# Sliding-window attention on one core: one TensorE visit per query tile, scores on row halves

## The chip, the cores and the metric

The kernel runs on one core of a Trainium2 chip. The metric is the device time of one execution in microseconds (us). TensorE (PE) takes its instructions in the order in which they are recorded; each engine has such a queue of its own, and engines wait for one another by semaphores.

## What is computed

One step of a two-layer decoder trunk: layer 0 is a gated linear recurrence, layer 1 sliding-window attention with sinks. The change touches layer 1 alone. Its core in the reference:

```python
def sink_attention(q, k, v, mask, sinks):
    s = jnp.einsum('bnqhgd,bnshd->bnhgqs', q, k) * SWA_SCALE
    s = jnp.where(mask[None, :, None, None], s, -jnp.inf)
    sink = sinks.astype(jnp.float32)[None, None, :, :, None, None]
    m = jnp.maximum(jnp.max(s, axis=-1, keepdims=True), sink)
    p = jnp.exp(s - m)
    p = p / (jnp.sum(p, axis=-1, keepdims=True) + jnp.exp(sink - m))
    return jnp.einsum('bnhgqs,bnshd->bnqhgd', p, v)
```

There are 32 query heads of 64 dimensions and 4 key heads. The prompt has 272 positions (16 of them meta tokens) with a window of 128; the sample group has 8 sequences of 8 new positions, each against 128 cached keys and its own 8. All numbers are f32. Layer 1 projects to q, k, v and a gate (2048 x 4608), attends, multiplies by SiLU of the gate and projects back.

## The kernel before, in words

`Stream` records the whole program in one order. Its main loop (`run`) goes through the weight matrices in tiles of 128 output columns, each tile in 4 chunks of 4 weight blocks. For each block it records three projection matmuls (L212 to L214: low weights by high inputs, high by low, high by high, all at full f32r rate) and then calls `step`, which advances at most two of the waiting side chains. A side chain is a Python generator: `yield 4` means that its next part is recorded 4 steps later at the earliest. So everything that is not a projection is strewn between the projections, at distances given by these yields. A tile is 16 steps, or 48 projection matmuls.

Weights come by DMA on the SP queue, 512 KB for two chunks, up to 14 chunks ahead (`raw`); ScalarE makes the rounded high part (L158), VectorE the rest (L169). Those conversions are recorded some chunks ahead.

In layer 1 the tiles are k0, k1, v0, v1, 16 query tiles (two heads each), 16 gate tiles. When query tile j is through, `epi_qq` starts `prompt_chain(j)`: `unfold` (scale and shift), a split into f32r parts `qh`, `ql`, three matmuls each for the first 128 queries (`sa`, 2 x 144 keys) and the others (`sb`, 2 x 256 keys), `softmax` on VectorE and ScalarE, eight transposes of the probabilities (L1056 to L1060), copies to SBUF (`t1`, `t2`), the outputs (`ao`, L1071 to L1077) and a copy into `oT`. The two heads of a tile share one key head; so that one matmul gives both heads' scores over all 128 rows, `kzh`, `kzl`, `knz`, `kzs` hold the keys twice, padded with zeros: half 0 on rows 0 to 63, half 1 on rows 64 to 127. Chains of neighbouring tiles overlap in time.

Twice per group of four tiles (one key head q), `sample_chain(q, u)` handles four of the eight sequences: it loads cached keys `cd` and values `cv`, transposes the keys (`ck`), copies them to `kzs`, computes scores (`ss`), softmax, transposes the probabilities (`st`) and makes outputs (`so`).

`tile_position` names the part of the 128 x 128 array that a matmul uses: `(0, 64 * h)` a half of its columns, `(0, 32 * i)` a quarter of them, `(64 * h, 0)` a half of its rows. A row half has its own 64 rows of weights and input and writes to a PSUM bank of its own. f32 matmuls run as two passes and appear as two instructions each. `pj`, `lv`, `mm` are the PSUM pools, with 3, 2 and 3 banks. `L["att"]` counts chains that run; the gate chains wait for it to be zero before they use `oT`.

## Time and profile before

| | |
|---|---|
| median of 3 runs | 1191.69 us (1191.45 to 1192.14) |
| profiled execution | 1193.07 us, span from first to last instruction 1191.3 us |
| granted TensorE clock, mean | 0.991 |
| instructions profiled | 26295, of them 10163 matmuls |

How to read it: the span is split by engine into busy times. Weight loads (PEld) overlap matmuls. A row of the timeline has the start from the beginning of the span, the length, engine, line, operation, tile written and tiles read, rows * columns of the array, shape and count of merged neighbours; in brackets the engine's idle time ahead and what ended it. Buffer numbers are left out of names.

### The profile page before, as it was taken

The page shows a single profiled execution, that of the slowest core. Times are in us where ns is not written, and L with a number is a line of the kernel's source. Part 1 is how long each engine was busy: PE and PEld are TensorE (multiplying, and loading weights), DVE is VectorE, ACT ScalarE, POOL GpSimd, SP SyncE. Part 2 cuts the span into 40 slices and gives each one's busy share as a digit, 9 for nine tenths or more (in the row PEclk, how much of TensorE's full clock was granted, in tenths as well). Part 3 has the DMA queues.
Part 4 walks back from the last instruction along what each step waited for, and adds up shares of the span by engine and source line. Part 5 has one row for each costly group of instructions (what it writes and reads, how often), then busy time and mean ns, then how long its engine had stood idle before and what let it go on. Part 6 is the DMA issues. An engine that isn't in the chain of part 4 may idle for free.

```text
span 1191.3 us, 26295 instructions
## 1 busy us (share of the span) xinstructions
PE 1170.4 (98%) x10163; PEld 1125.5 (94%) x10163; DVE 792.3 (67%) x2049; ACT 609.9 (51%) x1779; POOL 236.8 (20%) x350
## 2 busy tenths in 40 slices
PE   9999999999999999999999999999999999999995
PEld 7999999999999999999999999988888899999994
DVE  3765666565666565566578777678777767777675
ACT  4655545545555545555444446666656655553340
POOL 3022212212212212212224332000000011144420
PEclk8999999999999999999999999999999999999997
DMA  9545655445655545655455555634244345555532
GB/s 260 145 128 159 178 146 145 138 134 160 180 145 146 138 133 161 179 145 151 136 146 145 143 146 166 180 103 129 74 116 117 89 126 162 151 151 178 144 93 89
DMA packets 328462, 171.47 MB, mean 144 GB/s; under 512 B 19085, under 2 KB 325613, under 8 KB 328167
## 3 DMA queue, kind: packets, MB, share of 16 engines
q1 hardware_dynamic: 327792, 168.82, 50.2%
q8 instruction: 80, 1.31, 0.5%
q0 software_dynamic: 544, 0.97, 0.2%
q14 instruction: 46, 0.37, 0.1%
HBM read 156.97 MB, written 14.42 MB: 144 GB/s over the span
## 4 chain that ended last, share of the span: by engine, by line
PE 92%; issue 3%; DVE 2%; DMA 1%; ACT 1%; POOL 1%; SPq 0%; POOLq 0%; DVEq 0%; ACTq 0%
PE pj_q L212 7%; PE pj_g L212 7%; PE pj_g L213 7%; PE pj_g L214 6%; PE pj_q L213 6%; PE pj_q L214 6%; PE pj_f L212 4%; PE pj_i L212 3%; PE pj_i L214 3%; PE pj_i L213 3%; PE pj_f L214 3%; PE pj_f L213 3%; PE pj_z L214 3%; PE pj_z L213 3%; PE pj_z L212 3%
## 5 line engine op out<-in xcount | busy, mean ns | idle before, releaser
L212 PE MATMUL pj_q<-xh,wlo_q 128*128 128x336 f32 (+1 forms) x512 | 166.6, 325 | 0.0
L212 PE MATMUL pj_g<-xh,wlo_g 128*128 128x336 f32 (+1 forms) x512 | 162.9, 318 | 0.0
L213 PE MATMUL pj_q<-xl,whi_q 128*128 128x336 f32 (+1 forms) x512 | 161.2, 315 | 0.0
L214 PE MATMUL pj_q<-xh,whi_q 128*128 128x336 f32 (+1 forms) x512 | 160.9, 314 | 0.0
L213 PE MATMUL pj_g<-xl,whi_g 128*128 128x336 f32 (+1 forms) x512 | 160.6, 314 | 0.0
L214 PE MATMUL pj_g<-xh,whi_g 128*128 128x336 f32 (+1 forms) x512 | 160.4, 313 | 0.0
L212 PEld LDWEIGHTS pj_q<-xh,wlo_q 128*128 128x128 f32 x512 | 97.1, 190 | 5.8 <-issue 4.7
L212 PEld LDWEIGHTS pj_g<-xh,wlo_g 128*128 128x128 f32 x512 | 96.6, 189 | 1.5 <-issue 1.3
L213 PEld LDWEIGHTS pj_q<-xl,whi_q 128*128 128x128 f32 x512 | 97.3, 190 | 0.5
L214 PEld LDWEIGHTS pj_q<-xh,whi_q 128*128 128x128 f32 x512 | 97.1, 190 | 0.0
L213 PEld LDWEIGHTS pj_g<-xl,whi_g 128*128 128x128 f32 x512 | 96.8, 189 | 0.1
L214 PEld LDWEIGHTS pj_g<-xh,whi_g 128*128 128x128 f32 x512 | 96.6, 189 | 0.0
L169 DVE TENSOR_TENSOR wlo_g<-raw_g,whi_g 128x512 fp32r<-128x512 f32 x128 | 90.4, 743 | 0.6 <-ACT whi_g L158 0.6
L169 DVE TENSOR_TENSOR wlo_q<-raw_q,whi_q 128x512 fp32r<-128x512 f32 x128 | 85.1, 684 | 5.3 <-ACT whi_q L158 5.3
L212 PE MATMUL pj_f<-xh,wlo_f 128*128 128x336 f32 x256 | 83.7, 327 | 0.0
L213 PE MATMUL pj_f<-xl,whi_f 128*128 128x336 f32 x256 | 81.5, 318 | 0.0
L214 PE MATMUL pj_f<-xh,whi_f 128*128 128x336 f32 x256 | 81.5, 318 | 0.0
L212 PE MATMUL pj_i<-xh,wlo_i 128*128 128x336 f32 x256 | 81.4, 318 | 0.0
L212 PE MATMUL pj_z<-oh,wlo_z 128*128 128x336 f32 x256 | 81.3, 317 | 0.0
L214 PE MATMUL pj_z<-oh,whi_z 128*128 128x336 f32 x256 | 81.1, 317 | 0.0
L213 PE MATMUL pj_z<-ol,whi_z 128*128 128x336 f32 x256 | 81.0, 316 | 0.0
L213 PE MATMUL pj_i<-xl,whi_i 128*128 128x336 f32 x256 | 80.9, 316 | 0.0
(401 smaller groups left out, 3161.2 us busy)
## 6 DMA issues: line engine op xcount, KB each, us to landing
raw_g<-in_hgrn_w_in_dram SPq DMA_DIRECT2D x32, 512.0 KB
raw_z<-in_hgrn_w_out_dram SPq DMA_DIRECT2D x32, 512.0 KB
raw_q<-in_swa_w_in_dram SPq DMA_DIRECT2D x32, 512.0 KB
raw_g<-in_swa_w_in_dram SPq DMA_DIRECT2D x32, 512.0 KB
raw_y<-in_swa_w_out_dram SPq DMA_DIRECT2D x32, 512.0 KB
raw_f<-in_hgrn_w_in_dram SPq DMA_DIRECT2D x30, 512.0 KB
raw_q<-in_hgrn_w_in_dram SPq DMA_DIRECT2D x30, 512.0 KB
raw_i<-in_hgrn_w_in_dram SPq DMA_DIRECT2D x30, 512.0 KB
```

What stands on the lines that cost most here:

```text
L169: e.nc.vector.tensor_tensor(lo, t.pop(("raw", kc)), hi.bitcast(F32), op=ALU.subtract)
L212: nc.tensor.matmul(ps, lo[:, kk, :], xh, start=first, stop=False)
L213: nc.tensor.matmul(ps, hi[:, kk, :], xl, start=False, stop=False)
L214: nc.tensor.matmul(ps, hi[:, kk, :], xh, start=False, stop=last)
```

## The change

`prompt_chain` and `sample_chain` are gone. In their place stands `query_chain`, which after unfold and split makes one `visit(n)`. A visit records, one behind the other on TensorE: the scores of tile n, the transposes of the probabilities of tile n-1, transposes for a sample group if `plan` has some there (cached keys, or sample probabilities), the outputs of tile n-2 and sample outputs. Behind it come the softmax of n (`softmax_chain`) and the copies out of PSUM. After the last tile four visits (n = 16 to 19) finish the rest among the gate projections.

Keys are no longer padded: each half of the rows holds its own copy, and scores are pairs of matmuls, half h for head h, into two banks. Sample scores use eight parts of 64 rows by 32 columns. `vm0` has 128 rows (112 of them zero) instead of 16, `vs` 128 for each half instead of 64, so that all outputs use 128 rows by 64 columns; `t2` becomes two fixed tiles whose lower part is zeroed once. The sample probabilities lie in 384 neighbouring columns, three transposes instead of four. `ck` and `st` come from pool `pj` instead of `mm`. The yields in `softmax` are 3 and 3.

```diff
-            for nm, shape in (("vm1", [P, 256]), ("vm2", [P, 256]), ("vm0", [16, 256]), ("vs", [NS, 256]),
+            for nm, shape in (("vm1", [P, 256]), ("vm2", [P, 256]), ("vm0", [P, 256]), ("vs", [P, 2, 256]),
                               ("km2", [P, 256]), ("ks", [NS, 256]),
                               ("sk", [P, 32]), ("sks", [P, 8])):
                 L[nm] = ap1.tile(shape, F32, tag=nm, name=nm)
+            for q in range(2):
+                L["t2", q] = ap1.tile([P, 512], F32, tag=f"t2_{q}", name=f"t2_{q}")
+            for t in (L["vm0"], L["vs"], L["t2", 0][:, 256:512], L["t2", 1][:, 256:512]):
+                nc.gpsimd.memset(t, 0.0)
...
             for q in range(4):
                 for nm in ("kzh", "kzl"):
-                    t = ap1.tile([P, 2, NP], F32R, tag=f"{nm}{q}", name=f"{nm}{q}")
-                    L[nm, q] = t
-                t = ap1.tile([P, 2, NS], F32, tag=f"knz{q}", name=f"knz{q}")
-                nc.gpsimd.memset(t, 0.0)
-                L["knz", q] = t
+                    L[nm, q] = ap1.tile([P, NP], F32R, tag=f"{nm}{q}", name=f"{nm}{q}")
+                L["knz", q] = ap1.tile([P, NS], F32, tag=f"knz{q}", name=f"knz{q}")
                 L["qs", q] = ap1.tile([P, 8, 4, 8], F32, tag=f"qs{q}", name=f"qs{q}")
             for q in range(2):
-                t = ap1.tile([P, 4, 2, P], F32, tag=f"kzs{q}", name=f"kzs{q}")
-                nc.gpsimd.memset(t, 0.0)
-                L["kzs", q] = t
-            def zeros():
-                yield 20
-                for q in range(4):
-                    for nm in ("kzh", "kzl"):
-                        nc.scalar.copy(L[nm, q][0:64, 1, :], zero[0:64, :])
-                        nc.scalar.copy(L[nm, q][64:128, 0, :], zero[64:128, :])
-                        yield 4
-            st.spawn(zeros())
+                L["kzs", q] = ap1.tile([P, 4, P], F32, tag=f"kzs{q}", name=f"kzs{q}")
...
-            yield 4
+            yield 3
             for c, pt in enumerate(parts):
...
-            yield 3 if nm is not None else 4
+            yield 3
...
-            yield 5 if nm is not None else 4
...
-        def prompt_chain(j, pq):
+        def query_chain(j, pq):
...
+            yield from visit(j, (qh, ql))
+            if j == KT - 1:
+                for n in range(KT, KT + 4):
+                    yield (8, 1, 4, 1)[n - KT]
+                    yield from visit(n)
+                L["att"] = 0
+        plan = {}
+        for q in range(4):
+            for u in range(2):
+                n = 4 * q + 3 + u
+                plan.setdefault(n - 1, {})["load"] = q, u
+                plan.setdefault(n, {})["keys"] = q, u
+                plan.setdefault(n + 2 - u * (q == 3), {})["trans"] = q, u
+                plan.setdefault(n + 3 - u * (q == 3), {})["out"] = q, u
+        plan[18]["trans"] = 3, 1
+        plan[17]["trans"] = 3, 0
+        plan[18]["out"] = 3, 0
+        plan.setdefault(19, {})["out"] = 3, 1
+        def visit(n, qq=None):
+            ap = L["ap"]
+            todo = plan.get(n, {})
+            while 0 < n <= KT and ("p", n - 1) not in L:
+                yield 0
+            while "trans" in todo and ("sp",) + todo["trans"] not in L:
+                yield 0
+            if n < KT:
+                qh, ql = qq
+                kh, kl = L["kzh", n // 4], L["kzl", n // 4]
+                pa = [lv.tile([P, 512], F32, tag="lv", name=f"s{c}{n}") for c in "ab"]
+                for o, w, t0, k0 in ((0, 144, 0, 0), (144, 256, 128, 16)):
+                    for i, (a, b) in enumerate(((ql, kh), (qh, kl), (qh, kh))):
+                        for h in range(2):
+                            r = halves2[h]
+                            nc.tensor.matmul(pa[h][:, o:o + w], a[r, t0:t0 + 128], b[r, k0:k0 + w], start=i == 0,
+                                             stop=i == 2, tile_position=(64 * h, 0), skip_group_check=True)
+            j = n - 1
+            if 0 <= j < KT:
+                sm = L["p", j]
+                p1, p2 = pm(f"p1_{j}"), pm(f"p2_{j}")
+                for h in range(2):
+                    nc.tensor.transpose(p1[:, 256 * h:256 * h + 128], sm[:, h, 16:144], ident)
+                    nc.tensor.transpose(p1[:, 256 * h + 128:256 * h + 256], sm[:, h, 144:272], ident)
+                for h in range(2):
+                    nc.tensor.transpose(p2[:, 128 * h:128 * h + 128], sm[:, h, 272:400], ident)
+                    nc.tensor.transpose(p2[0:16, 256 + 128 * h:384 + 128 * h], sm[:, h, 0:16], ident)
+            px = None
+            for kind in ("keys", "trans"):
+                if kind in todo:
+                    q, u = todo[kind]
+                    px = e.pj.tile([P, 512], F32, tag="pj", name=f"{'ck' if kind == 'keys' else 'st'}{q}_{u}")
+                    if kind == "keys":
+                        cd = L["cd", u]
+                        for i in range(4):
+                            nc.tensor.transpose(px[:, 128 * i:128 * i + 128], cd[:, i].rearrange("p h d -> p (h d)"),
+                                                ident)
+                    else:
+                        for i in range(3):
+                            nc.tensor.transpose(px[:, 128 * i:128 * i + 128],
+                                                L["sp", q, u][:, 128 * i:128 * i + 128], ident)
+            po = None
+            j2 = n - 2
+            if j2 >= 0:
+                po = pm(f"ao{j2}")
+            if 0 <= j2 < KT:
+                vs = slice(64 * (j2 // 4), 64 * (j2 // 4) + 64)
+                t1, t2 = L["t1", j2], L["t2", j2 % 2]
+                for v, t, c0, o, w in (("vm1", t1, 0, 0, 256), ("vm2", t2, 0, 128, 128), ("vm0", t2, 256, 0, 128)):
+                    for h in range(2):
+                        nc.tensor.matmul(po[halves2[h], o:o + w], L[v][:, vs], t[:, c0 + w * h:c0 + w * h + w],
+                                         start=v == "vm1", stop=v != "vm1", tile_position=(0, 64 * h),
+                                         skip_group_check=True)
+            if "out" in todo:
+                q, u = todo["out"]
+                vs = slice(64 * q, 64 * q + 64)
+                ts, cv = L["ts"], L["cv", u]
+                for h in range(2):
+                    nc.tensor.matmul(po[halves2[h], 256:384], L["vs"][:, h, vs], ts[:, 128:256], start=True,
+                                     stop=False, tile_position=(0, 64 * h), skip_group_check=True)
+                for i in range(4):
+                    for h in range(2):
+                        c = 256 * h + 32 * i
+                        nc.tensor.matmul(po[halves2[h], 256 + 32 * i:288 + 32 * i], cv[:, i, :], ts[:, c:c + 32],
+                                         start=False, stop=i == 3, tile_position=(0, 64 * h), skip_group_check=True)
+            yield 1
+            if n < KT:
+                st.spawn(softmax_chain(n, pa))
+            if 0 <= j < KT:
+                t1 = ap.tile([P, 512], F32, tag="t1", name=f"t1_{j}")
+                t2 = L["t2", j % 2]
+                L["t1", j] = t1
+                nc.scalar.copy(t1, p1)
+                nc.scalar.copy(t2[:, 0:256], p2[:, 0:256])
+                nc.scalar.copy(t2[0:16, 256:512], p2[0:16, 256:512])
+            if "keys" in todo:
+                q, u = todo["keys"]
+                nc.scalar.copy(L["kzs", u].rearrange("p b k -> p (b k)"), px)
+            if 0 <= j2 < KT:
+                nc.scalar.copy(L["oT"][:, j2, 0:256], po[:, 0:256])
+            if "out" in todo:
+                q, u = todo["out"]
+                nc.vector.tensor_copy(
+                    L["oT"][:, 4 * q:4 * q + 4, 256 + 32 * u:288 + 32 * u].rearrange("p j (b t) -> p j b t", t=8),
+                    po[:, 256:384].rearrange("p (b j t) -> p j b t", j=4, t=8))
+            if "trans" in todo:
+                ts = ap.tile([P, 384], F32, tag="ts", name=f"ts{n}", bufs=1)
+                L["ts"] = ts
+                nc.scalar.copy(ts, px[:, 0:384])
+            if "load" in todo:
+                yield 3
+                q, u = todo["load"]
+                cd = ap.tile([P, 4, 2, 64], F32, tag="cd", name=f"cd{q}_{u}")
+                for half in range(2):
+                    nc.sync.dma_start(cd[:, :, half, :],
+                                      cache_k[0, 4 * u:4 * u + 4, :, q, :].rearrange("b s d -> s b d"))
+                cv = ap.tile([P, 4, 64], F32, tag="cv", name=f"cv{q}_{u}")
+                nc.sync.dma_start(cv, cache_v[0, 4 * u:4 * u + 4, :, q, :].rearrange("b s d -> s b d"))
+                L["cd", u], L["cv", u] = cd, cv
+            if "keys" in todo:
+                yield 4
+                yield from sample_scores(*todo["keys"])
+        def softmax_chain(n, pa):
+            ap = L["ap"]
+            sm = ap.tile([P, 2, 400], F32, tag="sm", name=f"sm{n}")
+            stat = ap.tile([P, 16], F32, tag="stat", name=f"stat{n}")
+            for h in range(2):
+                nc.vector.scalar_tensor_tensor(sm[:, h, :], pa[h][:, 0:400], 0.125, cst[:, 8:408], op0=ALU.mult,
+                                               op1=ALU.add)
...
+            parts = [sm[:, h, o:o + w] for o, w in ((0, 144), (144, 256)) for h in range(2)]
+            yield from softmax(stat, parts, sink4.rearrange("p a h -> p (a h)"))
+            L["p", n] = sm
+        def sample_scores(q, u):
...
+            ps = [lv.tile([P, 512], F32, tag="lv", name=f"ss{c}{q}_{u}") for c in "ab"]
+            for own in range(2):
+                for i in range(4):
+                    for h in range(2):
+                        r = halves2[h]
+                        o, w = ((0, 64)[h], 128) if not own else ((128, 0)[h], 64)
+                        nc.tensor.matmul(ps[h][32 * i:32 * i + 32, o:o + w], qs[r, 4 * u + i],
+                                         knz[r, :] if own else L["kzs", u][r, i], start=True, stop=True,
+                                         tile_position=(64 * h, 32 * i), skip_group_check=True)
+            yield 1
...
+            def rest():
+                yield from softmax(stat, [sm[:, 192 * h:192 * h + 192] for h in range(2)],
+                                   L["sks"][:, 2 * q:2 * q + 2])
+                L["sp", q, u] = sm
+            st.spawn(rest())
```

What this moves on TensorE. First the scores of query tile 15 before (`sa`, `sb`, then the cached keys of a sample group):

```order
L1039 MATMUL sa_12795<-kzh_10089,ql_12761 128x288
L1040 MATMUL sa_12795<-kzl_10090,qh_12760 128x288
L1041 MATMUL sa_12795<-kzh_10089,qh_12760 128x288
L1039 MATMUL sb_12796<-kzh_10089,ql_12761 128x512
L1040 MATMUL sb_12796<-kzl_10090,qh_12760 128x512
L1041 MATMUL sb_12796<-kzh_10089,qh_12760 128x512
L1095 MATMUL ck_1_12803<-ident,cd_1_12696 128x128 x4
```

and the scores of tile 7 now:

```order
L1058 MATMUL sa_11618<-kzh_10083,ql_11599 128x144
L1058 MATMUL sb_11619<-kzh_10083,ql_11599 128x144
L1058 MATMUL sa_11618<-kzl_10084,qh_11598 128x144
L1058 MATMUL sb_11619<-kzl_10084,qh_11598 128x144
L1058 MATMUL sa_11618<-kzh_10083,qh_11598 128x144
L1058 MATMUL sb_11619<-kzh_10083,qh_11598 128x144
L1058 MATMUL sa_11618<-kzh_10083,ql_11599 128x256
L1058 MATMUL sb_11619<-kzh_10083,ql_11599 128x256
L1058 MATMUL sa_11618<-kzl_10084,qh_11598 128x256
L1058 MATMUL sb_11619<-kzl_10084,qh_11598 128x256
L1058 MATMUL sa_11618<-kzh_10083,qh_11598 128x256
L1058 MATMUL sb_11619<-kzh_10083,qh_11598 128x256
```

Six matmuls with 2 x 144 or 2 x 256 columns became twelve with 144 or 256, `sa` for the lower rows and `sb` for the upper. Next the outputs of tile 14 before, with the projections (`pj_g`) and the sample scores around them:

```order
L1071 MATMUL ao_12965<-t_14_12923,vm_10064 64x256 x2
L1074 MATMUL ao_12965<-t_14_12924,vm_10065 64x128 x2
L1077 MATMUL ao_12965<-t_14_12924,vm_10066 64x128 x2
L212 MATMUL pj_g_1_12961<-xh_91,wlo_g_1_3_12870 128x322
L213 MATMUL pj_g_1_12961<-xl_107,whi_g_1_3_12824 128x322
L214 MATMUL pj_g_1_12961<-xh_91,whi_g_1_3_12824 128x322
L1105 MATMUL ss_0_12977<-knz_10091,qs_10093 128x128
L1109 MATMUL ss_0_12977<-kzs_10094,qs_10093 32x256 x4
```

and the second half of visit 7 now, behind the twelve scores above and five more transposes:

```order
L1069 MATMUL p_6_11632<-ident,sm_11518 16x128
L1068 MATMUL p_6_11633<-ident,sm_11518 128x128
L1069 MATMUL p_6_11633<-ident,sm_11518 16x128
L1078 MATMUL ck_0_11642<-ident,cd_0_11538 128x128 x4
L1093 MATMUL ao_11647<-t_5_11505,vm_10063 64x256 x2
L1093 MATMUL ao_11647<-t_1_10072,vm_10064 64x128 x2
L1093 MATMUL ao_11647<-t_1_10072,vm_10065 64x128 x2
L1101 MATMUL ao_11647<-ts_11511,vs 64x128 x2
L1106 MATMUL ao_11647<-ts_11511,cv_1_11020 64x32 x8
L212 MATMUL pj_q_8_11534<-xh_87,wlo_q_8_2_11389 128x322
```

Transposes, outputs and sample outputs now follow one another with no projection between them, and the next projection comes behind all of them. Last the end of the attention now, visits 18 and 19 among the projections of gate tile 2:

```order
L1082 MATMUL st_1_13319<-ident,sms_1_13251 128x128 x3
L1101 MATMUL ao_13323<-ts_13285,vs 64x128 x2
L1106 MATMUL ao_13323<-ts_13285,cv_0_12905 64x32 x8
L212 MATMUL pj_g_2_13215<-xh_86,wlo_g_2_2_13080 128x322
L213 MATMUL pj_g_2_13215<-xl_102,whi_g_2_2_12977 128x322
L214 MATMUL pj_g_2_13215<-xh_86,whi_g_2_2_12977 128x322
L212 MATMUL pj_g_2_13215<-xh_87,wlo_g_2_2_13080 128x322
L213 MATMUL pj_g_2_13215<-xl_103,whi_g_2_2_12977 128x322
L214 MATMUL pj_g_2_13215<-xh_87,whi_g_2_2_12977 128x322
L1101 MATMUL ao_13347<-ts_13342,vs 64x128 x2
L1106 MATMUL ao_13347<-ts_13342,cv_1_13067 64x32 x8
```

Before, 15 projections stood between the last `st` and the `so` that uses it; now the outputs of another group and six projections do.

More of the change, by code (lines that the diff above doesn't have):

```diff
@@ L1050, in prompt_chain @@
-            sink4 = ap.tile([P, 2, 2], F32, tag="sink4", name=f"sink4_{j}")
-            nc.gpsimd.tensor_copy(sink4, L["sk"][:, 2 * j:2 * j + 2].unsqueeze(1).to_broadcast([P, 2, 2]))
-            parts = [sm[:, h, o:o + n] for o, n in ((0, 144), (144, 256)) for h in range(2)]
-            yield from softmax(sm, stat, parts, sink4.rearrange("p a h -> p (a h)"), j)
-            p1, p2 = pm(f"p1_{j}"), pm(f"p2_{j}")
-            for h in range(2):
-                nc.tensor.transpose(p1[:, 256 * h:256 * h + 128], sm[:, h, 16:144], ident)
-                nc.tensor.transpose(p1[:, 256 * h + 128:256 * h + 256], sm[:, h, 144:272], ident)
@@ L1103, in sample_chain @@
-            yield 7 + 8 * u
-            ps = lv.tile([P, 512], F32, tag="lv", name=f"ss{q}_{u}")
-            nc.tensor.matmul(ps[:, 256:384], qs[:, 4 * u:4 * u + 4].rearrange("p b j t -> p (b j t)"), knz,
-                             start=True, stop=True, skip_group_check=True)
-            for i in range(4):
-                b = 4 * u + i
-                nc.tensor.matmul(ps[32 * i:32 * i + 32, 0:256], qs[:, b], L["kzs", u][:, i], start=True, stop=True,
-                                 tile_position=(0, 32 * i), skip_group_check=True)
@@ L1111, in sample_chain @@
-            yield 1
-            sm = ap.tile([P, 2, 400], F32, tag="sm", name=f"sms{q}_{u}")
-            stat = ap.tile([P, 16], F32, tag="stat", name=f"stats{q}_{u}")
-            for n, m0, o, src in ((128, 408, 0, 0), (64, 536 + 64 * u, 128, 256)):
-                nc.vector.scalar_tensor_tensor(
-                    sm[:, :, o:o + n], ps[:, src:src + 2 * n].rearrange("p (h k) -> p h k", h=2), 0.125,
-                    cst[:, m0:m0 + n].unsqueeze(1).to_broadcast([P, 2, n]), op0=ALU.mult, op1=ALU.add)
@@ new lines, in sample_scores @@
+            yield 1
+            sm = ap.tile([P, 384], F32, tag="sms", name=f"sms{q}_{u}")
+            stat = ap.tile([P, 16], F32, tag="stats", name=f"stats{q}_{u}")
+            for h in range(2):
+                for w, m0, o in ((128, 408, (0, 64)[h]), (64, 536 + 64 * u, (128, 0)[h])):
+                    nc.vector.scalar_tensor_tensor(sm[:, 192 * h + o:192 * h + o + w], ps[h][:, o:o + w], 0.125,
+                                                   cst[:, m0:m0 + w], op0=ALU.mult, op1=ALU.add)
```

126 lines of the change are left out of this document (22 added, 104 removed).

## The prediction

> **What bounds the kernel now.** I read the page first, then the stage in which the changed lines run, then the order of single TensorE instructions there.
>
> ```profile
> PE 1170.4 (98%) x10163; PEld 1125.5 (94%) x10163; DVE 792.3 (67%) x2049; ACT 609.9 (51%) x1779; POOL 236.8 (20%) x350
> PE 92%; issue 3%; DVE 2%; DMA 1%; ACT 1%; POOL 1%; SPq 0%; POOLq 0%; DVEq 0%; ACTq 0%
> ```
>
> TensorE is busy for 98% of the span and makes 92% of the chain that ended last. A matmul's end is modelled, so what one costs is read from the distance of starts, below. The changed lines run between about 755 and 975 us; next come the stretch view of that stage for TensorE (length; busy time and instructions; granted clock; DMA) and the same for the matmuls that write `pj_q` and `pj_g` alone.
>
> ```profile
> 755.00:975.00 220.00, 219.34 (x1671) 1.00 0.39 110
> 755.00:975.00 220.00, 121.70 (x719) 1.00 0.39 110
> 755.00:975.00 220.00, 37.40 (x232) 1.00 0.39 110
> ```
>
> The clock is full, so nothing is to be had or lost there. The stage is 719 + 232 = 951 projection matmuls and the attention's between them. This is the timeline of TensorE (start, length) at the places that carry prices:
>
> ```profile
> 804.94 0.31 PE L212 MATMUL pj_q<-xh,wlo_q 128*128 128x322 f32 x1
> ...
> 805.68 0.31 PE L214 MATMUL pj_q<-xh,whi_q 128*128 128x322 f32 x1
> 805.92 0.65 PE L1071 MATMUL ao<-t,vm 128*64 128x256 f32 x4
> 806.40 0.39 PE L1074 MATMUL ao<-t,vm 128*64 128x128 f32 x4
> 806.72 0.43 PE L1077 MATMUL ao<-t,vm 16*64 16x128 f32 x4
> 807.09 0.41 PE L212 MATMUL pj_q<-xh,wlo_q 128*128 128x322 f32 x1
> 807.33 0.31 PE L213 MATMUL pj_q<-xl,whi_q 128*128 128x322 f32 x1
> ...
> 807.63 0.27 PE L1123 MATMUL st<-ident,sms 128*128 128x128 f32 x1
> ...
> 808.22 0.31 PE L213 MATMUL pj_q<-xl,whi_q 128*128 128x322 f32 x1
> ...
> 808.96 0.29 PE L1039 MATMUL sa<-kzh,ql 128*128 128x288 f32 x1
> ...
> 809.36 0.39 PE L1039 MATMUL sb<-kzh,ql 128*128 128x512 f32 x1
> ...
> 810.06 0.31 PE L212 MATMUL pj_q<-xh,wlo_q 128*128 128x322 f32 x1
> ...
> 811.24 0.32 PE L214 MATMUL pj_q<-xh,whi_q 128*128 128x322 f32 x1
> 811.48 0.44 PE L1132 MATMUL so<-ts,vs 64*64 64x128 f32 x4
> 811.85 0.66 PE L1137 MATMUL so<-ts,cv 128*64 128x32 f32 x16
> 812.44 0.41 PE L212 MATMUL pj_q<-xh,wlo_q 128*128 128x322 f32 x1
> 812.69 0.31 PE L213 MATMUL pj_q<-xl,whi_q 128*128 128x322 f32 x1
> ```
>
> Five projection matmuls take 805.68 - 804.94 = 0.74, one 0.148; 951 of them are 141 us, so attention costs TensorE 220 - 141 = **79.0 us**. Its parts, each from a row to the next projection row less the projections between:
>
> - scores of a tile (`sa`, `sb`): 810.06 - 808.96 = 1.10, times 16 = 17.6. A 288-column one takes 0.40/3 = 0.133, a 512-column one 0.70/3 = 0.233: 0.45 ns a column, so 0.07 for 144 columns and 0.12 for 256.
> - outputs (`ao`): 807.33 - 805.68 - 0.30 = 1.35, times 16 = 21.7.
> - sample outputs (`so`): 812.69 - 811.24 - 0.30 = 1.15, times 8 = 9.2; sample transposes (`st`): 808.22 - 807.63 - 0.15 = 0.44, four at 0.11, times 8 = 3.5; cache-key transposes (`ck`), four as well, 3.5.
> - transposes of a tile and sample scores, from these rows: 819.60 - 818.57 - 0.15 = 0.88, times 16 = 14.1; 798.32 - 797.03 - 0.30 = 0.99, times 8 = 7.9.
>
> ```profile
> 797.03 0.31 PE L214 MATMUL pj_q<-xh,whi_q 128*128 128x322 f32 x1
> 797.18 0.38 PE L1105 MATMUL ss<-knz,qs 128*128 128x128 f32 x2
> 797.50 0.64 PE L1109 MATMUL ss<-kzs,qs 128*32 128x256 f32 x8
> ...
> 798.32 0.31 PE L213 MATMUL pj_q<-xl,whi_q 128*128 128x322 f32 x1
> ...
> 818.57 0.27 PE L1056 MATMUL p<-ident,sm 128*128 128x128 f32 x1
> ...
> 819.60 0.31 PE L213 MATMUL pj_q<-xl,whi_q 128*128 128x322 f32 x1
> ```
>
> These make 77.5; the other 1.5 us are waits, such as this one, 0.68 where a projection takes 0.15:
>
> ```profile
> 869.11 0.30 PE L214 MATMUL pj_q<-xh,whi_q 128*128 128x322 f32 x1
> 869.79 0.63 PE L1095 MATMUL ck<-ident,cd 128*128 128x128 f32 x4 [0.38 <-DVE sm L1046]
> ```
>
> **What a change of layout costs.** The columns `128*64` and `16*64` tell which part of the array an instruction uses; two halves run side by side (16 matmuls of `so` in 0.59). From L214 at 805.68 to `ao` at 805.92 are 0.24, 0.09 more than a projection: the array empties. The four 256-column ones take 0.48 where two rounds of two passes (0.107 per 128 columns, as the transposes) make 0.43: 0.05 for weights that nothing hides. Into column halves: 0.15. L1074 to L1077 takes 0.32 for 0.21, L1077 to L212 0.37 for 0.21: the step from 128 to 16 rows is 0.10 of emptying and 0.05 of loading, the way back 0.10, and L212 to L213 adds 0.10 (0.24 for 0.15) for 128 columns of weights. Back to the full array: 0.20. `so` pays the same three.
>
> **The change, part by part.**
>
> *Scores on row halves.* Six matmuls over zero-padded keys become six pairs on 64 rows each (three of 144 columns, three of 256), in separate PSUM banks. By stream alone a tile is 3 x 0.07 + 3 x 0.12 = 0.57. Loads bound it too: a 128-column load follows another after 0.11 in this weight-load timeline.
>
> ```profile
> 554.45 0.19 PEld L212 LDWEIGHTS pj_f<-xh,wlo_f 128*128 128x128 f32 x1
> 554.55 0.19 PEld L213 LDWEIGHTS pj_f<-xl,whi_f 128*128 128x128 f32 x1
> ```
>
> So I take 3 x 0.11 + 3 x 0.12 = 0.69, if the halves' loads and matmuls run side by side. No row shows 64-row halves; the nearest are the 5- and 10-row matmuls at the end, on three row strips, in these stretches of L1314 (TensorE, then weight loads, then the clock):
>
> ```profile
> 1179.30:1180.08 0.78, 0.59 (x3) 0.51 (x6) 0.50 0.00 0
> 1180.08:1180.50 0.42, 0.42 (x6) 0.33 (x2) 0.50 0.56 215
> ```
>
> At half clock a 512-column matmul needs twice 0.233, 0.47; three stand in the first stretch of 0.59 with the next three's loads, and the next three start in the second. Strips do run side by side. Bounds: 0.57 (stream alone) and 1.38 (one half after the other). Going into row halves and out again I price like a return to the full array, 0.20 each (full-width weights); bounds 0.10 and 0.35. Scores alone thus go from 1.10 to 1.09: nothing.
>
> *One visit.* A regular tile (n = 2 to 15) is 0.20 + 0.69 + 0.20 + transposes 0.88 + 0.15 + outputs 0.855 + 0.20 = 3.18 against 1.10 + 0.88 + 1.35 = 3.33. The outputs lose the step to 16 rows (`vm0` is padded to 128): 2 x 0.213 + 4 x 0.107 = 0.855. n = 0 is 1.09, n = 1 is 1.97, n = 16 2.09, n = 17 1.21, and 18 and 19, with sample outputs alone, 0.15 + 0.70 + 0.20 = 1.05 each. Together 14 x 3.18 + 8.5 = 53.0.
>
> *Samples.* `so` moves into visits, with no layout change of its own in six of eight: 2 x 0.107 + 0.49 (L1137's 16: 0.59 less 0.10 of emptying) = 0.70, 4.2 in all; the other two are in n = 18, 19. `st` has three transposes for four: 0.33, times 8 = 2.6. `ck` stays 3.5. Scores run on eight tiles of 64 rows by 32 columns: 0.09 + 0.03 (loads of 32 columns) + two passes of 128 (0.21) + two of 64 (0.11) + 0.20 = 0.64, times 8 = 5.1; bounds 0.5 and today's 0.99.
>
> Sum after: 53.0 + 4.2 + 2.6 + 3.5 + 5.1 = 68.4, against 79.0: **-10.6 us**.
>
> *Waits.* Inside a visit TensorE stands before the transposes of n-1 if its probabilities are late, and all projections behind them stand too. On VectorE today:
>
> ```profile
> 771.76 0.68 DVE L1046 SCALAR_TENSOR_TENSOR sm<-sb,cst 128x512 f32<-128x512 f32 x1
> ...
> 778.34 1.06 DVE L1020 TENSOR_SCALAR sm<-sm,stat 128x144 f32<-128x144 f32 x4
> ```
>
> From the last scores to the last normalization are 7.6 us (to 779.4). In the change the rest of a visit (0.20 + 0.88 + 0.15 + 0.855 + 0.20 = 2.3), 48 projections (7.1) and the next scores (0.9) lie between: 10.3. So 2.7 to spare, and the waits of today go. At the end they come back once: visit 18 transposes the last sample's probabilities directly behind their normalization.
>
> ```profile
> 948.27 0.62 DVE L1115 SCALAR_TENSOR_TENSOR sms<-ss,cst 128x256 f32<-128x256 f32 x2 [1.35 <-PE p L1060]
> ...
> 952.49 0.55 DVE L1020 TENSOR_SCALAR sms<-sms,stats 128x192 f32<-128x192 f32 x2
> ```
>
> Today 4.8 us, with the 1.35 ahead 6.1; in the change 27 projections (4.0) and visit 17 (1.5) lie between, 5.5. I charge 0.6, between 0 and 2.5. ScalarE takes over the 16 small copies of VectorE; these are both kinds today, the mean in ns behind the comma:
>
> ```profile
> L1066 DVE COPY t<-p 16x256 f32<-16x256 f32 x16 | 6.6, 410 | 11.7 <-ACT t L1065 11.7
> L1064 ACT COPY t<-p 128x512 f32<-128x512 f32 x16 | 9.4, 585 | 14.4 <-PE p L1057 14.4
> ```
>
> 16 x 0.41 more on ScalarE lies beside TensorE: it is busy for 51%. The cache loads (24 DMAs of 128 KB on SP) go out 13 steps before their use plus part of a visit, against 12: hidden as before; without that cover each of eight visits would wait the 3 to 4 us that 384 KB take at the 110 GB/s above. The SP queue's weight loads behind them keep their lead, since no slot they need is still in use. Zero copies that vanish (ScalarE, about 740 us) lie beside a TensorE that does not wait.
>
> Total -10.6 + 0.6 = -10.0. The profiled execution took 1193.07 (span 1191.3), the median is 1191.69; so **1181.7** for the median.
>
> **Rivals.** (1) *The halves run one after the other*: 1.38 for 0.69, +11.0: 1192.7, no change. Against it are the strips of L1314, which are 32 rows high and not 64. 6%. (2) *Weights of a half are loaded only when its own matmul is through*: pairs of 0.11 + 0.07 and 0.11 + 0.12, 1.23 for 0.69, +8.6: 1190.3, no change. Against it: on full rows a load lasts 0.19 (554.45) and a projection starts every 0.148, so loads do lie beside matmuls on the same rows, and in L1314's first stretch six loads lie beside three matmuls. 5%. The Trainium skill states this rule (TensorE: Matmul & The Clock Gate, Part 3, "The mechanism"): loads overlap matmuls in flight only where the row group differs. Here the trace disagrees, with its 0.19 and 0.148. (3) *Slower: late probabilities.* ScalarE gets four to five copies behind each visit (0.4 to 0.6 each, by the two rows above) ahead of the exponentials; if the 7.6-us chain grows past 10.3, all of TensorE waits once per tile. From 0.63 us a tile on (10.0/16) it is slower than before; at 1.0 it gives 1197.7. For it: today's first tiles wait; against: 2.7 us to spare, VectorE's wait of 1.35 above. 8%. (4) *Dearer layouts*: into and out of row halves 0.35 each, +4.8: 1186.5. 12%, half of it beside other small losses up to 1189.
>
> **How the numbers follow.** The forecast case (69%) spans scores 0.57 to 0.75, layout changes 0.10 to 0.25 and end waits of 0 to 2.5: 1177 to 1185. With rival 4 the range goes to 1188. What a measurement of this kernel can tell is 0.2%, 2.4 us: faster means under 1189.3, which holds the forecast and rival 4, 81%; the same 11% (rivals 1 and 2); slower 8%.
>
> **What would show it.** Right: L1058's twelve matmuls in about 0.7 us, halves starting together; about 3.2 us from the last projection before a regular visit to the first behind it; attention at 68 to 69 us of the stage. Wrong: L1058 pairs 0.2 us apart (rivals 1, 2); L1065 waiting on L1005 (rival 3); more than 0.25 at L1058 or L1065 with no wait on another engine (rival 4); or a stage as short as said and a span that is not, the gain lost behind 975 us.

## The result, and the profile after

The changed kernel takes 1206.2 us (median of 4, 1202.6 to 1206.5) against 1191.9 before: ratio 1.011, 95% interval 1.009 to 1.013. The forecast was 1181.7, range 1177 to 1188. The profiled execution took 1206.5, its span is 1204.7.

The page's busy times and its chain of waits, which answer to the first lines of the prediction:

```profile
PE 1167.5 (97%) x10427; PEld 1127.2 (94%) x10427; DVE 785.3 (65%) x2026; ACT 603.3 (50%) x1765; POOL 234.0 (19%) x348
PE 85%; DVE 7%; issue 3%; ACT 2%; DMA 1%; POOL 1%; SPq 0%; POOLq 0%; DVEq 0%; ACTq 0%
```

TensorE holds 85% of the chain in place of 92%, VectorE 7% in place of 2%. The same stretch as in the prediction, for the matmuls of `pj_q` and of `pj_g`, says how much:

```profile
755.00:975.00 220.00, 110.01 (x704) 104.12 (x702) 8.20 (x15) 2.19 (x15) 0.96 0.38 105
755.00:975.00 220.00, 23.40 (x145) 21.68 (x146) 1.09 (x2) 0.28 (x2) 0.96 0.38 105
```

By the prediction's own measure (141 us for 951 projections, 0.1483 each), 849 projections make 125.9, so attention now costs TensorE 220 - 125.9 = **94.1 us**. Before it was 79.0, forecast was 68.4. The granted clock has fallen too: 0.96, where it was full. The waits of this stretch (engine, line, waited for; us in all, times, longest):

```profile
PE sa L1058 <- DVE ql L265: 17.4, 9, 3.1
DVE oT L1125 <- ACT oT L1122: 31.9, 6, 5.7
```

TensorE waits nine times, always ahead of a visit's first matmul, for `ql`, the low part of the next tile's queries. No row has the transposes L1065 waiting for the probabilities. Before, VectorE had the first sign of the second row, at the copy of the sample outputs:

```profile
DVE oT L1142 <- PE so L1137: 5.5, 3, 3.5
```

How the two waits hang together is read from one place, visits 6 and 7. Visit 6 in TensorE's timeline (first and last scores, the last outputs), then VectorE's, then ScalarE's:

```profile
821.71 0.33 PE L1058 MATMUL sa<-kzh,ql 64*128 64x144 f32 x1
...
822.39 0.28 PE L1058 MATMUL sb<-kzh,qh 64*128 64x256 f32 x1
...
825.08 0.61 PE L1106 MATMUL ao<-ts,cv 128*64 128x32 f32 x16
```

```profile
826.14 0.29 DVE L1125 COPY oT<-ao 128x128 f32<-128x128 f32 x1 [4.97 <-ACT oT L1122]
826.35 0.68 DVE L169 TENSOR_TENSOR wlo_q<-raw_q,whi_q 128x512 fp32r<-128x512 f32 x1
826.95 0.57 DVE L1151 SCALAR_TENSOR_TENSOR sm<-sa,cst 128x400 f32<-128x400 f32 x1
...
831.65 0.55 DVE L872 SCALAR_TENSOR_TENSOR un_q<-nmb,gb_q,pj_q 128x320 f32<-128x320 f32 x1 [1.43 <-ACT gb_q L870]
...
834.63 0.41 DVE L265 TENSOR_TENSOR ql<-qf,qh 128x256 fp32r<-128x256 f32 x1
```

```profile
825.73 0.37 ACT L1122 COPY oT<-ao 128x256 f32<-128x256 f32 x1 [1.34 <-PE ao L1106]
...
829.58 0.42 ACT L999 ACTIVATE sm<-sm,stat 128x144 f32<-128x144 f32 x1 [2.58 <-DVE stat L995]
...
831.48 0.14 ACT L870 COPY gb_q<-pj_q 128x2 f32<-128x2 f32 x1
```

The scores are there at 822.7. But VectorE has come to L1125, which is recorded ahead of the softmax (L1151) and copies sample outputs, the last thing that the visit makes. It stands 4.97 us, until L1122 is through, which in its turn waits for the last outputs (L1106). The softmax starts 4.3 us late; the exponentials wait for it; and L870, the first step of tile 7's query split, stands behind them on ScalarE. From there L872, L265 and the scores of visit 7 follow:

```profile
832.68 0.32 PE L214 MATMUL pj_q<-xh,whi_q 128*128 128x322 f32 x1
835.19 0.30 PE L1058 MATMUL sa<-kzh,ql 64*128 64x144 f32 x1 [2.19 <-DVE ql L265]
...
836.34 0.42 PE L1066 MATMUL p<-ident,sm 128*128 128x128 f32 x1
836.56 0.42 PE L1065 MATMUL p<-ident,sm 128*128 128x128 f32 x1
...
840.82 0.41 PE L212 MATMUL pj_q<-xh,wlo_q 128*128 128x322 f32 x1
```

TensorE stands 2.4 us (835.19 - 832.68 - 0.15), and a second loss follows: the transposes behind start every 0.22 in place of 0.11, at half clock. The stretches around it show the granted clock (before the last two columns), first ahead of visit 7, then around visits 7 and 8:

```profile
755.00:820.00 65.00, 62.69 (x536) 57.80 (x535) 50.08 (x144) 41.90 (x132) 2.58 (x13) 1.00 0.45 127
820.00:840.00 20.00, 17.81 (x151) 15.96 (x152) 8.96 (x24) 9.09 (x26) 0.43 (x2) 0.91 0.37 100
840.00:860.00 20.00, 16.93 (x190) 14.90 (x185) 13.79 (x42) 11.13 (x39) 0.43 (x2) 0.91 0.36 99
```

Sample outputs stand in visits 6, 7, 10, 11, 14 and 15; the visits behind the first five of these, 7, 8, 11, 12 and 15, are the dear ones: 8.0 to 8.3 us. Visits 5, 9 and 13 wait some 1.3, visit 1 some 1.0, without half clock.

### The profile page after: what moved, and what is told of

Same layout as the page of the kernel before. It is cut to its first block, busy times and chain, and to the rows that moved or that the text cites. A ratio compares the mean times of both kernels' runs of the same rounds, so it can differ in the third digit from the quotient of the medians.

```text
span 1204.7 us, 26781 instructions
## 1 busy us (share of the span) xinstructions
PE 1167.5 (97%) x10427; PEld 1127.2 (94%) x10427; DVE 785.3 (65%) x2026; ACT 603.3 (50%) x1765; POOL 234.0 (19%) x348
## 4 chain that ended last, share of the span: by engine, by line
PE 85%; DVE 7%; issue 3%; ACT 2%; DMA 1%; POOL 1%; SPq 0%; POOLq 0%; DVEq 0%; ACTq 0%
PE pj_g L212 6%; PE pj_g L213 6%; PE pj_g L214 6%; PE pj_q L212 5%; PE pj_q L213 5%; PE pj_q L214 5%; PE pj_f L212 4%; PE pj_i L212 3%; PE pj_f L214 3%; PE pj_f L213 3%; PE pj_i L214 3%; PE pj_i L213 3%; PE pj_z L214 3%; PE pj_z L213 3%; PE pj_z L212 3%
## 5 line engine op out<-in xcount | busy, mean ns | idle before, releaser
L212 PE MATMUL pj_q<-xh,wlo_q 128*128 128x336 f32 (+1 forms) x512 | 163.2, 319 | 0.0
```

Source lines behind the costliest of these rows:

```text
L212: nc.tensor.matmul(ps, lo[:, kk, :], xh, start=first, stop=False)
```

## The experiments

Theory A: L1125's place in VectorE's order makes the softmax late, L870's place behind the exponentials carries that to the query split, and the waits bring the clock down. Rivals: the query chain is too long for its 12 steps anyway (B); dense visits bring the clock down, not waits (C); L1125 loads VectorE, wherever it stands (D). In the table "stage" is the measure used above, 220 us less 0.1483 for each projection in 755 to 975; visits are costed like the parts in the prediction, from the last projection ahead to the second behind, less two. Each ratio is to the kernel before as measured beside that run (1191.8 to 1192.8 us).

| run | time, us | ratio to before (95%) | stage | visit 1 | 5 | 7 | 8 |
|---|---|---|---|---|---|---|---|
| before | 1191.9 | | 79.0 | | | | |
| changed | 1206.2 | 1.009 to 1.013 | 94.1 | 2.94 | 4.77 | 8.06 | 8.3 |
| L1125 on ScalarE | 1187.1 | 0.995 to 0.997 | 73.2 | 2.93 | 4.77 | 4.22 | 3.79 |
| L1125 later on VectorE | 1188.5 | 0.995 to 0.998 | 73.3 | 2.93 | 4.76 | 4.28 | 3.57 |
| exponentials later | 1189.3 | 0.995 to 0.998 | 75.1 | 2.08 | 3.67 | 5.26 | 5.20 |
| visits later | 1188.3 | 0.995 to 0.999 | 74.8 | 6.37 | 3.45 | 4.29 | 4.20 |
| L1125 on ScalarE, visits later | 1187.1 | 0.994 to 0.997 | 74.4 | 6.42 | 3.44 | 4.21 | 3.56 |
| the same, visit 0 early | 1184.0 | 0.991 to 0.995 | 68.4 | 1.92 | 3.45 | 4.21 | 3.56 |
| the same, scores on full rows | 1182.7 | 0.990 to 0.994 | 69.5 | 1.97 | 3.51 | 4.28 | 3.62 |
| before, scores on row halves | 1192.5 | 0.998 to 1.002 | 78.4 | | | | |

### L1125 on ScalarE

```diff
-                nc.vector.tensor_copy(
+                nc.scalar.copy(
                     L["oT"][:, 4 * q:4 * q + 4, 256 + 32 * u:288 + 32 * u]...
```

> The copy of the sample outputs (L1125) moves from VectorE to ScalarE, behind L1122; nothing else changes. Theory A (VectorE, in order, stands in L1125 until the visit's last outputs are through, the softmax starts 4 us late, and the next tile's query split with it): the long waits before visits 7, 8, 11, 12 and 15 go, and the half clock behind them; those five visits fall from 8.0-8.3 us to between 3.6 and 5.4 us, L1151 starts within 1 us of the scores' end in every visit, and the time is 1206.2 - 5 x 4.3 = 1185, at most 1191 if each of the five keeps the 1.2 us that visits 5, 9 and 13 wait. Rival B (the query chain is too long for its 12 steps anyway, because the copy L870 stands behind the exponentials on ScalarE): the waits stay or move, time over 1198. Rival C (the clock falls because a visit packs TensorE more densely, not because it waits): the granted clock of the stretches around the five visits stays at 0.91, and about half of the loss, 10 us, stays: about 1196.

VectorE's row at the same visit 6, and TensorE's wait in the stage:

```profile
822.23 0.57 DVE L1151 SCALAR_TENSOR_TENSOR sm<-sa,cst 128x400 f32<-128x400 f32 x1 [0.93 <-PE sb L1058]
```

```profile
PE sa L1058 <- DVE ql L265: 5.0, 6, 1.2
```

The softmax follows the scores at once, the five long waits and the half clock behind them are gone, and 19 us of the 21 forecast with them. C falls: visits are as dense as before, at full clock. B falls for the five long waits; what stays is the small wait ahead of 1, 5, 9 and 13, and in these the chain may indeed be too long for its 12 steps: at 5, 9 and 13 it goes when the visits come later (below).

### L1125 later, on VectorE

```diff
-                nc.vector.tensor_copy(L["oT"]..., po...)
+                def late(q=q, u=u, po=po):
+                    yield 3
+                    nc.vector.tensor_copy(L["oT"]..., po...)
+                st.spawn(late())
```

> The changed kernel with L1125 left on VectorE and recorded 3 steps later, behind the scaling, the maxima and the statistics of the visit's softmax. Theory A (its place in VectorE's order, ahead of the softmax, makes the loss): the five long waits go as they do with the copy on ScalarE, visits 7, 8, 11, 12 and 15 cost 3.6 to 5.4 us, time 1187 within 3. Rival D (the load on VectorE makes it: 0.4 us of copy at the wrong moment, wherever it stands): over 1198.

1188.5, visits 7 and 8 at 4.28 and 3.57. TensorE's waits in the stage are down to the four small ones:

```profile
PE sa L1058 <- DVE ql L265: 4.7, 4, 1.3
```

It is the place, not the engine's load: D falls.

### The exponentials later on ScalarE

```diff
             nc.vector.tensor_tensor(sks, sink, mxs, op=ALU.subtract)
-            yield 3
+            yield 5
             for c, pt in enumerate(parts):
                 nc.scalar.activation(pt, pt, AF.Exp, ...)
```

> The changed kernel with one number changed: the exponentials (L999) are recorded 5 steps behind the maxima in place of 3, so that the copy L870 of the next tile's unfolding stands ahead of them on ScalarE, where it stood behind them. L1125 stays on VectorE, ahead of the softmax, and the visit keeps its 3 steps. If L870's place behind the exponentials is the second link of the chain: L870 goes some 2 us earlier, the split (which still follows the exponentials through L876) about 1.7 us earlier; in visits 7, 11 and 15 2.4 us of waiting become 0.7, in 8 and 12 3.2 become 1.5, no half clock: 1206.2 - 5 x (1.7 + 1.5) = 1190. If the blocked softmax alone holds the split up, whatever the order on ScalarE: 1203 to 1207, with L870 waiting less and L876 where it was.

L1125 still stands 5.22 us (4.97 without the edit), but on ScalarE L870 now runs ahead of the exponentials:

```profile
825.31 0.16 ACT L870 COPY gb_q<-pj_q 128x2 f32<-128x2 f32 x1 [0.25 <-PE pj_q L214]
827.63 0.42 ACT L999 ACTIVATE sm<-sm,stat 128x144 f32<-128x144 f32 x1 [2.16 <-DVE stat L995]
```

```profile
824.19 0.29 DVE L1125 COPY oT<-ao 128x128 f32<-128x128 f32 x1 [5.22 <-ACT oT L1122]
...
831.44 0.42 DVE L265 TENSOR_TENSOR ql<-qf,qh 128x256 fp32r<-128x256 f32 x1 [0.25 <-ACT qh L264]
```

From L1125 to L265 are 7.2 us; in the changed kernel they were 8.5. About 1.0 to 1.6 us of waiting stays at each of the five visits, too short for half clock, and 1189.3 stands for the 1190 expected. So the second link is shown as well: either of the two places in an order, once mended, takes away most of the loss.

### Visits later

```diff
             nc.gpsimd.tensor_copy(L["qs", q]..., qf[:, 256:320]...)
-            yield 3
+            yield 6
             yield from visit(j, (qh, ql))
```

> L1125 stays on VectorE. The wait of the query chain before its visit grows from 3 steps to 6, so each visit is recorded 9 projections (1.3 us) later, and the copy L870 of the next tile then stands ahead of the exponentials on ScalarE, where it stood behind them. Theory A (the wait is for the query split, which is late because everything behind L1125 is late, L870 among it): the small waits before visits 1, 5, 9 and 13 (1.0 to 1.2 us) go; of the five long ones (3 us of waiting each, and 1.3 to 1.7 at half clock) most goes, since 1.3 us come from the steps and about 2 us from L870 no longer standing behind five exponentials; L1125 itself still waits about 5 us on VectorE. Time 1181 to 1187. If the order on ScalarE has no part in it, 1.3 of 3.0 us go at each of the five and 1.7 stay, without half clock: about 1190. Rival C (dense visits bring the clock down): no better than 1196.

> Both edits: L1125 on ScalarE, and the visit 3 steps later. Theory A: no wait for the query split is left, visits cost 3.2 to 4.2 us, and the stage's attention comes to the 68.4 us of the sum plus small waits: 1180 to 1183. If the late probabilities of the prediction's third rival now decide (ScalarE has L1125's 0.4 us more and the exponentials later), L1065 waits and the time is 1184 to 1190. Rival C: 1196 with a granted clock under 1 around the visits.

With L1125 left where it is, VectorE stands nearly as long (first row), yet TensorE waits long only once, ahead of visit 1 (second); ahead of visits 8 and 12 it waits 0.6:

```profile
DVE oT L1125 <- ACT oT L1122: 26.7, 6, 5.4
PE sa L1058 <- DVE ql L265: 2.7, 1, 2.7
```

The times, 1188.3 and 1187.1, miss the 1181 to 1187 and 1180 to 1183 expected, because of visit 1, which no theory had. ScalarE in the run with both edits:

```profile
765.30 0.62 ACT L158 CAST whi_q<-raw_q 128x512 fp32r<-128x512 f32 x1 [4.98 <-DMA raw_q<-in_swa_w_in_dram]
765.93 1.28 ACT L999 ACT_TABLE_LOAD   x1
767.23 0.42 ACT L999 ACTIVATE sm<-sm,stat 128x144 f32<-128x144 f32 x1
```

A weight conversion waits 4.98 us for its DMA; later visits put the first exponentials, and the split behind them, in the queue behind it. The table load that comes with the first exponentials stands there too, 1.28 us; in the changed kernel it runs at 756.79, where ScalarE then waits anyway. The same kind of loss, on another engine.

### Visit 0 early

```diff
-            yield 6
+            yield 3 if j == 0 else 6
```

> As the run with both edits (L1125 on ScalarE, visits 3 steps later), but visit 0 stays at 3 steps. In that run visit 1 alone still cost 6.42 us, 2.80 of it a wait for the query split: a weight conversion (L158) on ScalarE waited 4.98 us for its DMA and stood ahead of the exponentials of tile 0 and the split of tile 1. With visit 0 early, the exponentials of tile 0 stand ahead of that conversion, as they do in the changed kernel. Expected: visit 1 at 2.0 to 2.9 us, no wait for L265 of over 1.3 us, attention 68.6 us on TensorE (the prediction's sum was 68.4), time 1187.1 - 4.4 = 1182.7, 0.992 of before. If the wait of visit 1 moves to visit 2 with the DMA, the time stays near 1187.

Against the run with both edits visit 0 alone moves. The two rows of the stage (`pj_q`, `pj_g`), at full clock:

```profile
755.00:975.00 220.00, 109.20 (x701) 103.65 (x699) 8.17 (x15) 2.57 (x15) 1.00 0.42 118
755.00:975.00 220.00, 49.75 (x321) 47.67 (x322) 3.27 (x6) 0.94 (x6) 1.00 0.42 118
```

1022 projections make 151.6, attention 68.4, the prediction's sum (with 0.148 for a projection it would be 68.7, and 79.3 before); 0.8 us of it is a wait of a gate projection, `pj_g`, at 955. This version is faster than both kernels: 1184.0, ratio 0.991 to 0.995.

### What the row halves are worth

The kernel before with pairs on row halves and nothing merged:

```diff
-            for ps, n, t0, k0, k1 in ((pa, 288, 0, 0, 144), (pb, 512, 128, 16, 272)):
-                o = ps[:, 0:n]
-                ... three matmuls over kh[:, :, k0:k1], kl[:, :, k0:k1]
+            for o, w, t0, k0 in ((0, 144, 0, 0), (144, 256, 128, 16)):
+                for i, (a, b) in enumerate(((ql, kh), (qh, kl), (qh, kh))):
+                    for h, ps in enumerate((pa, pb)):
+                        r = slice(64 * h, 64 * h + 64)
+                        nc.tensor.matmul(ps[:, o:o + w], a[r, t0:t0 + 128], b[r, h, k0:k0 + w], ...,
+                                         tile_position=(64 * h, 0), ...)
```

> The kernel before with one part of the change: the six score matmuls of a tile become six pairs on row halves (the keys' zero halves stay in memory and are not read), and the scaling reads 400 columns of each half in place of two stretches of both; nothing is merged into a visit. The prediction's sum: 0.20 + 0.69 + 0.20 = 1.09 for 1.10 us per tile, so no change, 1191.9 within 2 us. If into and out of row halves cost 0.35 each, +4.8 us: 1196.5. If a layout change is nearly free (0.10 each way), -3.4: 1188.5. If the row halves, and not the visit, brought the loss or the half clock, it is slower by several us with a clock under 1.

```profile
807.99 0.31 PE L214 MATMUL pj_q<-xh,whi_q 128*128 128x322 f32 x1
808.23 0.33 PE L1041 MATMUL sa<-kzh,ql 64*128 64x144 f32 x1
808.24 0.33 PE L1041 MATMUL sb<-kzh,ql 64*128 64x144 f32 x1
...
809.12 0.42 PE L212 MATMUL pj_q<-xh,wlo_q 128*128 128x322 f32 x1
809.37 0.31 PE L213 MATMUL pj_q<-xl,whi_q 128*128 128x322 f32 x1
809.52 0.31 PE L214 MATMUL pj_q<-xh,whi_q 128*128 128x322 f32 x1
```

The pairs start together, and a tile costs 809.52 - 807.99 - 3 x 0.148 = 1.09: forecast 1.09, before 1.10. The time does not move, 1192.5. The other way round, the fast version with full rows (padded keys, six matmuls, `pa` holding both halves of 144 keys and `pb` of 256):

> As the run with visit 0 early, but with the scores on the full array again, over zero-padded keys (six matmuls of 288 and 512 columns, as in the kernel before), inside the same visits. By the prediction's prices a visit loses 0.20 into and 0.20 out of row halves and pays 1.10 for 0.69: no change, 1182.7 within 2. If the row halves carry part of the gain, it is slower by 4 us or more; if they cost, faster. The query split has one buffer for ql in place of two.

1182.7 and a visit 0.06 us dearer; against 1184.0 the intervals overlap. So the prompt scores on row halves carry none of the gain. Nor is all of it the merging. By the same way of costing, the regular work of the tiles falls by 3.2 us, the sample outputs inside visits by 3.2, the sample scores on 64 rows by 32 columns by 2.4 (8 times 0.99 less 0.69) and three sample transposes for four by 1.0; the rest are waits. These are estimates from the rows; no run takes the last two apart from the visits.

### The clock by itself

```diff
-            split(qh, ql, qf[:, 0:256])
+            nc.scalar.copy(qh, qf[:, 0:256])
+            for _ in range({3: 3, 6: 5, 9: 7, 12: 9, 14: 12}.get(j, 0)):
+                nc.vector.tensor_scalar(L["scr"], cst[:, 8:520], 1.0, None, op0=ALU.mult)
+            nc.vector.tensor_tensor(ql, qf[:, 0:256], qh.bitcast(F32), op=ALU.subtract)
```

> As the run with visit 0 early, with 3, 5, 7, 9 and 12 idle scalings of 128x512 on VectorE (about 0.6 us each; their results are used by nothing) ahead of the low part of the query split at visits 3, 6, 9, 12 and 14. TensorE should wait about 0.9, 2.1, 3.3, 4.5 and 6.3 us there (five lengths, one spoilt if a neighbour's wait runs into it). Theory: a wait of up to 1.4 us costs itself alone; from 2.4 us on (the shortest behind which the changed kernel shows half clock) it costs 1.2 to 1.7 us more, since the clock is half for some 3 us behind it, and not more the longer it lasts. 2.1 us tells which side it is on. Rival: the extra grows with the wait, to 3 us behind 6.3. Rival: no half clock behind any of them (it came from the visits' work): extra under 0.3.

A scaling took 0.43 us, not 0.6, and the split was some 2 us early, so the waits came out as 0, 0.1, 2.4, 2.4 and 3.5 us: the lengths between were missed. (One execution, 1196.2 us.) Visit 14, with TensorE's rows and then the stretches (clock before the last two columns):

```profile
921.80 0.31 PE L214 MATMUL pj_q<-xh,whi_q 128*128 128x322 f32 x1
925.42 0.30 PE L1062 MATMUL sa<-kzh,ql 64*128 64x144 f32 x1 [3.31 <-DVE ql L1022]
...
926.58 0.27 PE L1069 MATMUL p<-ident,sm 128*128 128x128 f32 x1
...
927.33 0.42 PE L1073 MATMUL p<-ident,sm 128*16 128x128 f32 x1
```

```profile
923.49:926.90 3.41, 1.48 (x17) 1.37 (x18) 3.31 (x9) 0.00 (x0) 0.00 (x0) 1.00 0.02 5
926.90:930.31 3.41, 3.41 (x24) 2.62 (x23) 2.58 (x8) 1.21 (x3) 0.00 (x0) 0.50 0.76 207
930.31:933.72 3.41, 3.41 (x38) 3.37 (x37) 1.59 (x3) 2.65 (x11) 0.00 (x0) 1.00 0.27 62
```

The visit costs 9.11 for 4.10 without the scalings; 3.47 (925.42 - 921.80 - 0.15) of the 5.01 is the wait, **1.54** the clock. The waits of 2.4 us at visits 9 and 12 cost 1.53 and 1.52 more than themselves. So the extra is the same behind 2.4 and 3.5 us, as the theory said and its rivals did not. It is not the same behind every wait, though: behind visit 1 of the run with both edits half clock lasts 6.8 us (770.88 to 777.70) in place of 3.4. Its attention costs 6.0 us more than with visit 0 early; 2.9 of that is the wait, so some 3.1 is the clock.

## Why the prediction was wrong

**The sum was right.** With 0.8 us of waits left, attention is 68.4 us against 68.4 forecast, and part by part: a regular visit 3.13 (forecast 3.18), with sample transposes and outputs 4.10 (4.21), with cache-key transposes 3.56 (3.62), sample scores 0.69 (0.64), n = 0 1.10 (1.09), n = 16 2.53 (2.53). Row halves run side by side (the two of a pair start together, the next pair 0.11 to 0.17 us later), and the layouts together cost no more than was taken: rivals 1, 2 and 4 fall. Inside the scores the terms were less right than their sum, which is in part luck: on row halves in the kernel before, the way in costs 0.09, the pairs and the way to the next projection 0.89 (809.12 - 808.23), that projection 0.10 extra, where 0.20 + 0.69 + 0.20 was forecast. The fast version's interval, 6 to 11 us under before, holds the forecast gain of 10.0.

**The step that failed is "Waits".** It followed one chain, scores to probabilities, by its durations of today, found 2.7 us to spare and concluded that "the waits of today go". Apart from 0.6 us at the end, waits stood in the sum at nothing; in the changed kernel they are 17.4 us, and the clock, on which the prediction said that nothing was to be had or lost, takes some 7.5 more. Two things were left out. First, the chain's durations hold only if nothing ahead of it in its queue waits longer; L1125 does, because a visit records 3 to 4 us of TensorE work in one piece and the copies of its end ahead of the softmax of its beginning. In the kernel before the same copy stood behind outputs of 1.15 us, with projections around, and still waited up to 3.5 us once: that row was there to be read. Second, the chain that ran out of time was the next tile's query split, which shares ScalarE and VectorE with the softmax; it was not followed at all. The probabilities themselves were never late.

**The size.** The row of TensorE's waits has 17.4 us in nine; five of them bring half clock, some 1.5 each by the clock run, 7.5 together. That is 24.9 of the 25.7 between 94.1 and 68.4. The span grew by 13.4 and not by 94.1 - 79.0 = 15.1, mostly because the two profiled executions differ in their first 100 us (clock 0.95 before, 1.00 after; the same matmul of layer 0, L684, stands at 593.04 and at 590.78). First before, then changed:

```profile
0.00:100.00 100.00, 97.32 (x844) 90.31 (x845) 57.75 (x158) 52.79 (x154) 20.63 (x48) 0.95 0.66 180
```

```profile
0.00:100.00 100.00, 98.60 (x858) 91.45 (x859) 59.98 (x162) 53.65 (x155) 20.68 (x48) 1.00 0.67 185
```

**Rival 3**, the slower one, had the right sign and the wrong place: it let late probabilities hold L1065, 8%, 1197.7 at 1.0 us a tile. Its sentence for ScalarE, that copies come ahead of the exponentials, was true of VectorE, and by position, not by load: ScalarE was busy for 50% and VectorE for 65%. The charge of 0.6 us at visit 18 was not needed (it costs 1.33 for 1.38 forecast).

## What to carry to other kernels

Where TensorE work is bundled and each engine takes its instructions in order, look at what the bundle puts ahead of what: a copy of the bundle's last result, recorded ahead of work on its first, holds everything behind it for the length of the bundle. Follow every chain that feeds the next bundle, not only the one that the change is about, and ask of each engine on it which instruction ahead can wait longest. A wait of TensorE of some 2 us or more should be charged with the half clock that it can bring, here 1.5 us behind most such waits and about 3 behind one; whether it comes depends on where the wait falls, which the next section shows.

## What the runs showed of the hardware

A wait of 2.4 us is enough to bring half clock, and it does not come with the wait: at visit 14 above the scores and the first transposes run at full pace for 1.5 us, then 3.41 us at 0.50. All ten such waits ahead of a visit (2.4 to 3.5 us; five in the changed kernel, one each in the two runs with visits later, three in the clock probe) had it; those of 1.7 us and less did not (the clock of the run with later exponentials is 1.00 throughout the stage). One wait of 2.8 us in the fast version, at 1065 us, did not have it either:

```profile
1065.04 0.31 PE L214 MATMUL pj_y<-ph,whi_y 128*128 128x320 f32 x1
1068.03 0.55 PE L1270 MATMUL yt<-ident,z 128*128 128x128 f32 x3 [2.68 <-DVE z L1260]
```

```profile
1062.88:1066.29 3.41, 2.47 (x17) 2.20 (x16) 0.92 (x3) 0.00 (x0) 0.16 (x1) 1.00 0.08 26
1066.29:1069.70 3.41, 1.67 (x12) 1.67 (x13) 2.97 (x10) 1.30 (x3) 2.08 (x2) 1.00 0.48 138
1069.70:1073.11 3.41, 3.41 (x26) 3.40 (x25) 3.41 (x10) 1.92 (x4) 2.13 (x3) 1.00 0.43 117
```

The records of the clock say what tells them apart. Within each trace, every change of the clock lies a whole number of 3.41 us from every other, in the changed kernel for instance at 836.09, 839.50, 853.16 and 856.57; where this grid stands differs from run to run. The stretches of 3.41 us shown here lie on it. TensorE's idle time in a stretch is its length less the first number behind it. The wait at 1065 is cut in two, 0.94 and 1.74 us, and neither part brings half clock; the stretch ahead of visit 14's half clock has 1.93. Over the eleven traces, from 20 us on and without the last 40 us, of the stretches at full clock all 14 with 1.93 us or more of idle time are followed by half clock, and none of the others, with 1.74 at most, is. So what counts is how much of a wait falls into one stretch of the grid, and half clock begins where that stretch ends: from 0.3 us before TensorE starts again (visit 1 of the runs with visits later) to 1.5 us after (visit 14). Behind eight of the ten waits it lasts one stretch, behind those of visit 1 two; why two is not shown.

The Trainium skill (TensorE: Matmul & The Clock Gate, Part 1, "What's actually happening") says that the clock halves after at least one idle window of about 3.4 us and comes back after a busy one of about as much, and that the windows run free of the kernel. The grid of 3.41 us agrees, and so does its place, which changes from run to run. A window idle from end to end was not needed: here 1.93 us of idling within one was enough, and the measurement decides.
